# Expert weight products in four column tiles, eight tokens at a time, in a hybrid decoder layer on one core

## The chip, the cores and the metric

The kernel runs on one core of a Trainium2 chip (trn2). The time is device microseconds of one execution, from the first to the last instruction with what lies around them. Three executions of the kernel before took 3187.74, 3201.39 and 3202.97 us, so the median is 3201.39 us. One more execution was profiled.

## The reference

One layer of a decoder trunk is computed for 512 prompt tokens and 64 sample tokens that share all weights: modulation from a condition, an input projection, a gated linear recurrence and a short convolution, an output projection, and then a product-key expert layer (PEER). The change lies in the last. Its core is:

```python
q = (xb @ w_q).reshape(PEER_BLOCK, PEER_HEADS, 2, HALF_DIM)
sc = jnp.einsum('thpk,pnk->thpn', q, sub_keys).astype(jnp.float32)
v1, i1 = lax.top_k(sc[:, :, 0], PEER_TOPK)
v2, i2 = lax.top_k(sc[:, :, 1], PEER_TOPK)
cand = (v1[..., :, None] + v2[..., None, :]).reshape(PEER_BLOCK, PEER_HEADS, PEER_TOPK * PEER_TOPK)
...
top, pos = lax.top_k(cand, PEER_TOPK)
eidx = jnp.take_along_axis(cidx, pos, axis=-1)
g = jax.nn.softmax(top, axis=-1).astype(xb.dtype)
act = jax.nn.gelu(jnp.einsum('td,thkd->thk', xb, expert_u[eidx])) * g
return jnp.einsum('thk,thkd->td', act, expert_v[eidx])
```

Every token picks 8 heads x 16 = 128 of 16384 experts; an expert is a row u and a row v of 2048 numbers. An expert's number is 128 x i1 + i2, so the experts lie in 128 blocks (one per i1) of 128 (one per i2).

## The kernel before

The prompt tokens' picks are treated in two ways. The 80 blocks (L = 80) that are picked most are computed densely: for each such block TensorE multiplies all 128 u rows with all 512 tokens. The picks in the other 48 blocks are gathered: POOL fetches, by an indirect DMA, one row per partition (`take`, L1235), and VectorE takes the dot product of it with the token's vector (L1263), or adds the v row with its weight to a sum (L1290). The sample tokens' picks are gathered too.

**The u stage.** A dense block's u rows come in two halves of 512 KB. `load` (L892) brings a half, `conv` splits it into a high part on ScalarE (xhi, L908) and a low part on POOL (xlo, L909), and `u_half` (L1395) multiplies: 8 slices of the inner dimension, three products each, 24 matmuls of 128 x 512, into one PSUM bank (pu). I call such a half a piece; there are 160, numbered n. After a block's second piece ScalarE applies the gelu and writes the block's activations to DRAM (L1408, L1409). The u banks are two and are taken in turn, so that one of them is idle while the other is filled.

**The weights of the dense picks.** A dense activation must be multiplied by the softmax weight of the token's pick, or by zero where the token did not pick that expert. These weights form, for each token, a matrix of 128 experts by 80 blocks, and TensorE makes it as a product over the token's 128 picks: `g_pair` (L1583) writes with two comparisons on VectorE (L1591), for eight tokens, a one-hot matrix of i2 (ops, 128 x 128) and one of the block (wr, 128 x 80); `g_scale` (L1599) multiplies ops by the picks' weights on ScalarE; `g_mm` (L1601) takes four tokens and makes four products into a PSUM bank (gbank, 4 x 80 columns), and `g_out` (L1608) copies the bank to SBUF on ScalarE (L1612). When 32 tokens are together, four DMAs write them to DRAM (gd); the v stage reads them back (gsb).

**The order.** From the last query projection on, the order on each engine is the one in which the code is written. A loop over the 160 pieces (L1643) writes, for each, the loads and splits of later pieces, one step of the weight work (`g_one`, `g_pair`, `g_scale`), then slot work on VectorE (which tells the rows of the next tile of tokens; steps1 and steps2) as long as a budget named `spare` is positive, then the row fetches and dot products that are due (`gather_to`), and then the matmuls of the piece. `spare` grows by PIECE_G per piece (PIECE before the weight work begins), and falls by 2.4 per row, 2.2 per `g_pair` and by each slot step's own cost. Rows can only be fetched for a tile whose slot work is written; from the piece at which the last slot work is written (R2), all rows that are left are spread evenly over the pieces that remain (L1695). `g_one` is called once at the start of a piece (L1653) and once in its middle, after 12 of its 24 matmuls, by `mid` (L1389, L1402).

**After the u stage** the v stage multiplies the weighted activations (actr, split into ahi and alo) with the v rows of the dense blocks (L1425), while the v rows of the other picks are gathered and added (L1290). Then come the final norm and the output.

## Time and profile before

| what | value |
|---|---|
| median of three runs | 3201.39 us (3187.74 to 3202.97) |
| the profiled execution | 3192.57 us |
| its span, first to last instruction | 3190.7 us |
| TensorE busy | 3063.3 us (96%) |
| VectorE busy | 2151.6 us (67%) |
| ScalarE, POOL busy | 1045.4 us (33%), 1708.0 us (54%) |
| moved by DMA | 882.84 MB, mean 277 GB/s |
| weight products (gbank, L1605) | 1525.5 to 2128.4 us, 1024 records |
| u pieces | up to about 2215 us |

The profile is of one execution. A row of a group gives engine, operation, output and inputs, the count, the busy time and the mean duration in ns, and then the idle time of the engine just before these instructions with what ended it. PE is a matmul and PEld the load of its stationary operand; a product of two f32 operands shows as two of each. Matmuls overlap, so the time from one start to the next tells more than a duration. A row of the timeline gives start and duration of equal neighbours taken together. A row of the waits gives who waited for whom, the sum, the times and the longest. The windows give each engine's busy time in a stretch, then the granted clock, the share of the DMA engines' time and the rate.

### The profile page before, as it was taken

How to read it: one execution, taken by the hardware profiler on the slowest of the kernel's cores; microseconds unless marked ns; L12 is line 12 of the kernel's file. 1: busy time of each engine (PE TensorE's matmuls, PEld its weight loads, DVE VectorE, ACT ScalarE, POOL GpSimd, SP SyncE). 2: the span in 40 equal slices, each digit the busy share in tenths (PEclk: the TensorE clock that was granted, in tenths of full speed). 3: DMA queues.
4: the chain of work that ended last, by engine and by line, in shares of the span. 5: the costliest groups of instructions: out<-in, count | busy, mean ns of one | idle time of the engine just before them, and what ended most of it. 6: DMA issues, size and time to landing. Idle time of an engine off the chain costs nothing.

```text
span 3190.7 us, 46633 instructions
## 1 busy us (share of the span) xinstructions
PE 3063.3 (96%) x17239; PEld 2604.8 (82%) x17239; DVE 2151.6 (67%) x3267; ACT 1045.4 (33%) x1640; POOL 1708.0 (54%) x1001
## 2 busy tenths in 40 slices
PE   6999999999989999999999999998999999999997
PEld 2788888889979998887888788886888888777776
DVE  3455521142245897977898999856677888788755
ACT  3244311122232232232655555542322222222122
POOL 2233333344334235666666666656767777768642
PEclk9999999999999999999999999999999999999998
DMA  9744566633332227889879898989999999899964
GB/s 391 279 137 138 177 215 215 205 121 132 130 121 90 70 83 247 307 312 399 339 309 402 354 400 354 403 281 357 395 376 383 401 341 367 329 397 344 368 245 155
DMA packets 297067, 882.84 MB, mean 277 GB/s; under 512 B 37590, under 2 KB 79446, under 8 KB 245366
## 3 DMA queue, kind: packets, MB, share of 16 engines
q1 hardware_dynamic: 160608, 380.39, 34.0%
q0 software_dynamic: 66336, 413.41, 32.5%
q10 hardware_dynamic: 69888, 86.00, 7.6%
q8 instruction: 136, 2.23, 0.3%
q14 instruction: 99, 0.81, 0.1%
HBM read 879.89 MB, written 66.81 MB: 297 GB/s over the span
## 4 chain that ended last, share of the span: by engine, by line
PE 74%; DMA 12%; DVE 5%; POOL 3%; issue 3%; ACT 1%; SPq 0%; ACTq 0%; POOLq 0%; DVEq 0%
PE pu L1405 20%; PE pv L1425 19%; PE pp_o L140 6%; DMA raw<-v 3%; PE pp_c L140 3%; PE pp_s L140 3%; PE qa L140 3%; PE pp_b L140 3%; PE qb L140 3%; DMA gsb<-gd 3%; PE pp_x L140 2%; PE pp_y L140 2%; PE ada L190 2%; PE gbank L1605 2%; DMA v<-v,rows 2%
## 5 line engine op out<-in xcount | busy, mean ns | idle before, releaser
L909 POOL TENSOR_TENSOR xlo<-raw,xhi 128x1024 fp32r<-128x1024 f32 x320 | 778.6, 2444 | 408.7 <-ACT xhi L908 403.0
L908 ACT ACTIVATE xhi<-raw 128x1024 fp32r<-128x1024 f32 x320 | 338.1, 1060 | 875.4 <-PE pv L1425 319.8
L1263 DVE SCALAR_TENSOR_TENSOR u<-u,hT 128x2048 f32<-128x2048 f32 x223 | 503.7, 2282 | 111.3 <-DMA u<-u,rows 110.0
L1290 DVE SCALAR_TENSOR_TENSOR accB<-v,dots,accB 128x2048 f32<-128x2048 f32 x211 | 496.5, 2353 | 109.4 <-DMA v<-v,rows 103.2
L1425 PE MATMUL pv<-ahi,xhi 128*128 128x512 f32 x1280 | 511.5, 400 | 23.1 <-ACT xhi L908 16.2
L1405 PE MATMUL pu<-hhi,xhi 128*128 128x512 f32 x1280 | 514.4, 402 | 0.0
L1425 PE MATMUL pv<-ahi,xlo 128*128 128x512 f32 x1280 | 508.3, 397 | 4.3 <-POOL xlo L909 4.3
L1425 PE MATMUL pv<-alo,xhi 128*128 128x512 f32 x1280 | 506.0, 395 | 0.0
L1405 PE MATMUL pu<-hhi,xlo 128*128 128x512 f32 x1280 | 502.7, 393 | 0.4 <-POOL xlo L909 0.3
L1405 PE MATMUL pu<-hlo,xhi 128*128 128x512 f32 x1280 | 502.9, 393 | 0.0
L1235 POOL DMA_INDIRECT u<-u,rows x223 | 224.8, 1008 | 211.1 <-DVE u L1263 142.4
L1425 PEld LDWEIGHTS pv<-ahi,xhi 128*128 128x128 f32 x1280 | 243.2, 190 | 80.5 <-ACT xhi L908 17.5
L1425 PEld LDWEIGHTS pv<-ahi,xlo 128*128 128x128 f32 x1280 | 243.1, 190 | 63.0 <-POOL xlo L909 6.2
L1425 PEld LDWEIGHTS pv<-alo,xhi 128*128 128x128 f32 x1280 | 243.6, 190 | 55.2
L1235 POOL DMA_INDIRECT v<-v,rows x223 | 258.1, 1157 | 54.7 <-issue 39.5
L1405 PEld LDWEIGHTS pu<-hhi,xlo 128*128 128x128 f32 x1280 | 240.8, 188 | 56.2 <-POOL xlo L909 2.1
L1405 PEld LDWEIGHTS pu<-hhi,xhi 128*128 128x128 f32 x1280 | 241.4, 189 | 49.4 <-issue 0.9
L1405 PEld LDWEIGHTS pu<-hlo,xhi 128*128 128x128 f32 x1280 | 241.5, 189 | 48.4
L1599 ACT ACTIVATE op<-op,it 128x128 f32<-128x128 f32 x512 | 155.3, 389 | 35.6 <-DVE op L1591 32.8
L1605 PEld LDWEIGHTS gbank<-wr,op 128*128 128x128 f32 x1024 | 133.5, 192 | 24.0 <-ACT stg L1612 15.0
L129 POOL TENSOR_TENSOR wlo_o<-raw_o,whi_o 128x1024 fp32r<-128x1024 f32 x32 | 77.6, 2425 | 119.7 <-ACT whi_o L127 119.7
L1447 DVE TENSOR_TENSOR acc<-acc,pv 128x512 f32<-128x512 f32 x144 | 96.4, 681 | 65.7 <-PE pv L1425 63.6
(498 smaller groups left out, 5439.4 us busy)
## 6 DMA issues: line engine op xcount, KB each, us to landing
wa<-w_ada SPq DMA_DIRECT2D x96, 1024.0 KB
raw<-ut SPq DMA_DIRECT2D x160, 512.0 KB
raw<-v SPq DMA_DIRECT2D x320, 256.0 KB
actd<-act ACTq DMA_DIRECT2D x80, 256.0 KB
gd<-stg ACTq DMA_DIRECT2D x64, 320.0 KB
gsb<-gd ACTq DMA_DIRECT2D x80, 256.0 KB
actr<-actd ACTq DMA_DIRECT2D x40, 512.0 KB
raw_o<-w_out SPq DMA_DIRECT2D x32, 512.0 KB
```

The source lines that it names most:

```text
L129: lo_engine(share).tensor_sub(lo, raw, r32(hi))
L140: PE.matmul(o, st, mv[pick](k), start=first, stop=last)
L908: S.activation(hi, raw, AF.Copy)
L909: G.tensor_sub(lo, raw, r32(hi))
L1235: G.indirect_dma_start(out=out, out_offset=None, in_=src, in_offset=bass.IndirectOffsetOnAxis(ap=idx, axis=0), bounds_check=NE * 128 - 1, ...
L1263: V.scalar_tensor_tensor(r, r, 1.0, st["h"], op0=ALU.mult, op1=ALU.mult, accum_out=dots[i][:, j:j + 1])
L1290: V.scalar_tensor_tensor(st["a"], r, dots[i][:, j:j + 1], st["a"], op0=ALU.mult, op1=ALU.add)
L1405: PE.matmul(pu, st[:, kk, :], movA[mv](k), start=k == 0 and a == 0, stop=k == KD - 1 and a == 2)
L1425: PE.matmul(pv, st, mv, start=first and j == 0 and a == 0, stop=last and not end and j == SG - 1 and a == 2)
L1447: V.tensor_add(ak, ak, pv)
L1599: S.activation(ops[:, j0 + j, :], ops[:, j0 + j, :], AF.Copy, scale=it[2][:, b * 4 + j:b * 4 + j + 1])
L1605: PE.matmul(pg[:, j * L:(j + 1) * L], ops[:, j0 + j, :], wr[:, j0 + j, :], start=True, stop=True)
```

## The change

`g_mm` now takes eight tokens. Each token's product is cut into four: 32 columns of ops are the stationary operand and the result goes to 32 output partitions, 32 products for eight tokens. The first four tokens go to a bank of their own, the u bank that the current block does not use, the other four to gbank. `pbank` names each bank explicitly so that a block and the weight products can ask for one by number. `g_out` copies both banks. `g_one` is no longer called at the start of a piece, only in its middle: after 12 matmuls in a block's first piece as before, after 6 in its second. PIECE_G, the budget per piece, is 6.3 instead of 6.9.

```diff
-PIECE_G = 6.9
+PIECE_G = 6.3
...
-    def pbank(tag, nm, bufs):
-        return psum["p"].tile([128, 512], F32, name=nm, tag=tag, bufs=bufs)
+    turns = {}
+
+    def pbank(tag, nm, bufs, at=None):
+        t = turns.get(tag, 0) if at is None else at
+        turns[tag] = t + 1
+        return psum["p"].tile([128, 512], F32, name=nm, tag=f"{tag}{t % bufs}", bufs=1)
...
-            fin["pu"] = pbank("u", f"pu{i}", 2)
+            fin["pu"] = pbank("u", f"pu{i}", 2, i)
...
-            if kk == 4:
+            if kk == (4, 2)[c]:
                 mid(n)
...
-    def g_mm(b):
-        ops, wr, j0 = pair.pop(b)
-        pg = gk["g"]
-        for j in range(4):
-            PE.matmul(pg[:, j * L:(j + 1) * L], ops[:, j0 + j, :], wr[:, j0 + j, :], start=True, stop=True)
-        return pg
-
-    def g_out(b, pg):
+    def g_mm(b, i):
+        ops, wr, _ = pair.pop(b)
+        pair.pop(b + 1)
+        gk["b"] = (pbank("u", f"gb{b}", 2, i + 1), gk["g"])
+        for j in range(8):
+            pg = gk["b"][j // 4][:, j % 4 * L:(j % 4 + 1) * L]
+            for q in range(0, 128, 32):
+                PE.matmul(pg[q:q + 32], ops[:, j, q:q + 32], wr[:, j, :], start=True, stop=True)
+
+    def g_out(b):
...
-        S.activation(stg[c][:, :, b0 * 4:b0 * 4 + 4].rearrange("p i t -> p t i"),
-                     pg[:, :4 * L].rearrange("p (t i) -> p t i", t=4), AF.Copy)
-        if b0 == TC // 4 - 1:
+        for h_, pg in enumerate(gk["b"]):
+            S.activation(stg[c][:, :, (b0 + h_) * 4:(b0 + h_) * 4 + 4].rearrange("p i t -> p t i"),
+                         pg[:, :4 * L].rearrange("p (t i) -> p t i", t=4), AF.Copy)
+        if b0 == TC // 4 - 2:
...
-        if n >= R1 + FIRST_G and gm[1] < min(upto(n - LAG), gm[2]):
-            g_out(gm[1], g_mm(gm[1]))
-            gm[1] += 1
+        if n >= R1 + FIRST_G and gm[1] + 1 < min(upto(n - LAG), gm[2]):
+            g_mm(gm[1], stream[n][1])
+            g_out(gm[1])
+            gm[1] += 2
             spare += 0.4
...
             put(2)
-            g_one(n)
             if not gk:
```

On TensorE, around the second piece of block 29 and the first of block 30 (pu29, pu30; xhi59 is the high part of piece 59, and the number behind a name is only its place in the program), the order before is:

```order
L1405 MATMUL pu29_14247<-hhi_78,xlo58_14136 128x512
L1605 MATMUL gbank_14007<-wr0_14090,op0_14089 128x80 x4
L1405 MATMUL pu29_14247<-hhi_78,xhi59_14181 128x512
...
L1405 MATMUL pu29_14247<-hhi_78,xlo59_14182 128x512
L1605 MATMUL gbank_14007<-wr0_14090,op0_14089 128x80 x4
L1405 MATMUL pu29_14247<-hhi_78,xhi59_14181 128x512
...
L1605 MATMUL gbank_14007<-wr2_14140,op2_14139 128x80 x4
L1405 MATMUL pu30_14394<-hhi_78,xhi60_14231 128x512
```

and with the change:

```order
L1409 MATMUL pu29_14247<-hhi_78,xlo59_14182 128x512
L1612 MATMUL gb0_14307<-wr0_14090,op0_14089 32x80 x16
L1612 MATMUL gbank_14007<-wr0_14090,op0_14089 32x80 x16
L1409 MATMUL pu29_14247<-hhi_78,xhi59_14181 128x512
...
L1409 MATMUL pu30_14397<-hhi_78,xhi60_14231 128x512
...
L1612 MATMUL gb2_14410<-wr2_14140,op2_14139 32x80 x16
L1612 MATMUL gbank_14007<-wr2_14140,op2_14139 32x80 x16
L1409 MATMUL pu30_14397<-hhi_78,xhi60_14231 128x512
```

Two sets of four tokens, at the start and in the middle of piece 59, became one set of eight after its first six matmuls; the next set comes after the first twelve of piece 60.

On POOL, near the end of the u stage (xlo155 is the low part of piece 155; u5 and v0 are gathered rows of the last tile of tokens and of the samples), the order before is:

```order
L909 TENSOR_TENSOR xlo155_20143<-raw155_20097,xhi155_20142 128x1024
L1235 DMA v0_9_20146<-v,rows0_8654 128x2048
L909 TENSOR_TENSOR xlo156_20190<-raw156_20137,xhi156_20189 128x1024
L1235 DMA v0_10_20193<-v,rows0_8654 128x2048
L1235 DMA v0_11_20198<-v,rows0_8654 128x2048
L909 TENSOR_TENSOR xlo157_20237<-raw157_20184,xhi157_20236 128x1024
L1235 DMA v0_12_20240<-v,rows0_8654 128x2048
L909 TENSOR_TENSOR xlo158_20280<-raw158_20231,xhi158_20279 128x1024
```

and with the change:

```order
L913 TENSOR_TENSOR xlo155_21700<-raw155_21649,xhi155_21699 128x1024
L1239 DMA v0_1_21703<-v,rows0_8654 128x2048
L1239 DMA v0_2_21708<-v,rows0_8654 128x2048
L1239 DMA v0_3_21713<-v,rows0_8654 128x2048
L913 TENSOR_TENSOR xlo156_21760<-raw156_21694,xhi156_21759 128x1024
L1239 DMA v0_4_21763<-v,rows0_8654 128x2048
L1239 DMA v0_5_21768<-v,rows0_8654 128x2048
L913 TENSOR_TENSOR xlo157_21807<-raw157_21754,xhi157_21806 128x1024
L1239 DMA v0_6_21810<-v,rows0_8654 128x2048
L1239 DMA v0_7_21815<-v,rows0_8654 128x2048
L1239 DMA v0_8_21820<-v,rows0_8654 128x2048
L913 TENSOR_TENSOR xlo158_21860<-raw158_21801,xhi158_21859 128x1024
```

The rows that stand between two low parts are two or three instead of one or two. Between xlo151 and xlo161 there are 27 (u5_0 to u5_10 and v0_0 to v0_15) instead of 13 (v0_4 to v0_16). By the planner's own numbers R2 is piece 149 instead of 131.

## The prediction

> **What bounds the kernel now.** I read the chain of waits of the page first, then the windows of the stretch that the change touches, then single instructions. A piece below is one half of a u block: 24 matmuls of L1405 with the work queued around them.
>
> ```profile
> PE 74%; DMA 12%; DVE 5%; POOL 3%; issue 3%; ACT 1%; SPq 0%; ACTq 0%; POOLq 0%; DVEq 0%
> PE pu L1405 20%; PE pv L1425 19%; PE pp_o L140 6%; DMA raw<-v 3%; PE pp_c L140 3%; PE pp_s L140 3%; PE qa L140 3%; PE pp_b L140 3%; PE qb L140 3%; DMA gsb<-gd 3%; PE pp_x L140 2%; PE pp_y L140 2%; PE ada L190 2%; PE gbank L1605 2%; DMA v<-v,rows 2%
> ```
>
> TensorE carries three quarters of the chain, and the matmuls that the change rewrites (gbank, L1605) stand in it with 2%. So a gain is possible, and it is at most some tens of us. Now the stretch with these matmuls (1520 to 2131), the u blocks left after it (2131 to 2215), the v stage, and three stretches inside the first, by the view of windows:
>
> ```profile
> core 0: us, PE busy (x) PEld busy (x) DVE busy (x) ACT busy (x) POOL busy (x), PEclk, DMA share, GB/s
> 1520.00:2131.00 611.00, 601.98 (x3113) 507.29 (x3112) 547.55 (x722) 351.07 (x765) 377.99 (x255) 0.99 0.90 356
> 2131.00:2215.00 84.00, 83.70 (x364) 67.77 (x363) 49.17 (x26) 20.88 (x23) 51.47 (x32) 1.00 0.95 361
> 2215.00:3100.00 885.00, 853.40 (x3662) 690.01 (x3660) 687.15 (x408) 207.53 (x197) 624.91 (x369) 0.98 0.96 361
> 1700.00:1760.00 60.00, 58.44 (x301) 48.33 (x300) 53.78 (x80) 33.85 (x73) 37.76 (x26) 1.00 1.02 420
> 1880.00:1940.00 60.00, 60.00 (x315) 51.06 (x314) 56.00 (x69) 36.36 (x82) 37.27 (x25) 1.00 1.02 421
> 2000.00:2060.00 60.00, 60.00 (x316) 51.06 (x315) 52.35 (x63) 36.48 (x83) 39.32 (x27) 1.00 1.02 419
> ...
> 1940.00:2000.00 60.00, 60.00 (x315) 51.06 (x314) 58.36 (x75) 33.79 (x74) 38.58 (x27) 1.00 0.85 333
> ```
>
> TensorE is busy 602 of 611 us, so it sets the pace. But it is not alone. In three stretches of 60 us the transfers run at 419 to 421 GB/s with a share of 1.02, and I take 421 GB/s as the most that this core gets; between them lie stretches like the last row's, at 333. VectorE is busy 547.6 of 611 us, and the view of waits of the same window says what it does in the rest:
>
> ```profile
> POOL u L1235 <- DVE u L1263: 128.8, 95, 4.3
> DVE u L1263 <- DMA u<-u,rows: 58.4, 40, 6.0
> PEld gbank L1605 <- ACT stg L1612: 15.0, 15, 3.7
> PE gbank L1605 <- ACT stg L1612: 8.9, 11, 3.3
> ```
>
> VectorE waits 58.4 us for gathered rows; 547.6 + 58.4 = 606 of 611, so it has hardly any free time either. POOL waits 128.8 us for VectorE to free a row buffer before it can fetch the next row. TensorE's own idle time, 9 us, is the 8.9 us before gbank. So three chains lie within some 2% of one another in this stretch: TensorE, VectorE with its rows, and in the dense stretches the transfers. What the change gives TensorE has to pass the other two.
>
> **The matmuls themselves.** What four tokens cost now, from the timeline (PE alone):
>
> ```profile
> 1709.04 0.39 PE L1405 MATMUL pu<-hlo,xhi 128*128 128x512 f32 x1
> 1709.27 0.39 PE L1405 MATMUL pu<-hhi,xlo 128*128 128x512 f32 x1
> 1709.50 1.01 PE L1605 MATMUL gbank<-wr,op 128*128 128x80 f32 x8
> 1710.30 0.48 PE L1405 MATMUL pu<-hhi,xhi 128*128 128x512 f32 x1
> 1710.62 0.39 PE L1405 MATMUL pu<-hlo,xhi 128*128 128x512 f32 x1
> ```
>
> A u matmul starts 0.23 us after the one before it (1709.04 to 1709.27). From 1709.27 to 1710.62 there are two such steps, 0.46 us, and the four tokens: 1.35 - 0.46 = 0.89 us. There are 128 such sets (1024 records, 8 a set): 114 us, and eight tokens cost 1.78 us.
>
> The new form, 32 columns of weights into one quarter of the output partitions, is not new to the trace: the ada products have it, with 512 moving columns. Its rows in the timeline, first the matmuls (PE), then the weight loads (PEld):
>
> ```profile
> 411.58 0.60 PE L200 MATMUL pm<-ident,part 128*128 128x128 f32 x4
> 412.11 1.92 PE L190 MATMUL ada<-wa,cpad 128*32 128x512 f32 x16
> 413.97 0.53 PE L140 MATMUL pp_b<-hhi,whi_b 128*128 128x288 f32 x2
> 414.33 0.42 PE L140 MATMUL pp_b<-hlo,whi_b 128*128 128x288 f32 x2
> 414.60 0.42 PE L140 MATMUL pp_b<-hhi,wlo_b 128*128 128x288 f32 x2
> ...
> 412.11 0.16 PEld L190 LDWEIGHTS ada<-wa,cpad 128*32 128x32 f32 x8 [0.17 <-issue]
> 412.57 0.13 PEld L190 LDWEIGHTS ada<-wa,cpad 128*32 128x32 f32 x4 [0.30 <-issue]
> 413.00 0.13 PEld L190 LDWEIGHTS ada<-wa,cpad 128*32 128x32 f32 x4 [0.30 <-issue]
> ```
>
> An f32 product is two passes, so the sixteen records, two products in four tiles each, are four passes of four tiles. The loads of one pass go out 0.43 us after those of the pass before (412.57, 413.00), and all four tiles share that time: they do run side by side. 0.43 us for 512 columns is 0.067 us for 80. Eight tokens are 16 passes (each f32 product has two): 1.07 us. Going in and out of the tiles costs something too. In: the loads idle 0.17 us, of which I count 0.1, and the first pass takes 0.46 instead of 0.43. Out: 413.97 is 0.54 after 413.00 + 0.43, which is 0.11 over a pass, and the next pair takes 0.36 instead of 0.27. That makes 0.33 us, and eight tokens 1.40 us. **Term 1: 64 x (1.78 - 1.40) = 24 us less on TensorE.** Bounds: 45 us less if going in and out cost nothing (64 x 0.71); nothing gained if a pass of short tiles takes as long as a pass of a whole array, 0.89 / 8 = 0.11 us, which 16 times is 1.78 again. I take the value between, since its parts are rows of the same form. No run of tiles in this trace is longer than 16, and here come 64 in a row; that is a rival below.
>
> [...]
>
> **Waits before gbank.** Two banks instead of one, filled once per piece, give ScalarE the rest of a piece to empty them. The cause of the 8.9 us stays, though: the copy (L1612) stands in ScalarE's queue behind the scaling of a later set, and this behind VectorE, which waits for rows. **Term 2: 4 us less** (0 to 9). The rows for this and for what follows: groups of instructions in the stretch with the tiles (two rows), after it (one), and from the page the queue of the gathered rows and their fetches.
>
> ```profile
> L1612 ACT ACTIVATE stg<-gbank 128x320 f32<-128x320 f32 x128 | 97.1, 759 | 14.5 <-PE gbank L1605 11.7 <-issue 2.6
> L1408 ACT ACTIVATE act<-pu 128x512 f32<-128x512 f32 x46 | 27.5, 599 | 121.4 <-PE pu L1405 120.1 <-issue 1.2
> ...
> L1290 DVE SCALAR_TENSOR_TENSOR accB<-v,dots,accB 128x2048 f32<-128x2048 f32 x12 | 28.2, 2354 | 18.1 <-DMA v<-v,rows 18.0
> ...
> q0 software_dynamic: 66336, 413.41, 32.5%
> ...
> L1235 POOL DMA_INDIRECT u<-u,rows x223 | 224.8, 1008 | 211.1 <-DVE u L1263 142.4
> L1235 POOL DMA_INDIRECT v<-v,rows x223 | 258.1, 1157 | 54.7 <-issue 39.5
> ```
>
> In the first half of a block the u bank still holds the block before. The tiles come 12 matmuls, 2.8 us, into the half, and the copy that empties that bank (L1408) takes 0.6 us. In the second half the u bank must be empty before the next block starts, 18 matmuls or 4.1 us after the tiles; two copies at 0.76 us (L1612) fit. Both hold while ScalarE isn't held up by a late row or raw tile; if it is, TensorE waits at the start of a block instead of before gbank. TensorE gets four times as many tile instructions; ScalarE keeps its 128 copies and VectorE its comparisons, and no DMA is added.
>
> **The dense stretches.** Shorter pieces ask for the same two rows in less time. In the three windows at 420 GB/s the transfers can't go faster, so the share of term 1 that falls there is lost: 24 x 180 / 611 = 7 us. **Term 3: 7 us back** (0, if the four rows in flight carry a stretch over, to 15, if the stretches are twice as long as my windows cut them).
>
> **What the smaller PIECE_G moves.** It changes no instruction, but the plan: with 6.3 instead of 6.9 the table grants the slot work less, so tiles of rows come ready later, and the last of them are gathered at the end of the u stage. By POOL's order, between the low halves of pieces 151 and 161 there stand 27 row fetches instead of 13. Those pieces are the 84 us after 2131, where 361 GB/s x 84 us = 30.3 MB move already. A row is 1.05 MB if all 128 partitions are in use; the mean over the kernel is 413.41 MB / 446 row fetches (223 + 223 on L1235) = 0.93 MB. 14 more rows are 13 MB, 43.3 MB in all, and at 421 GB/s 103 us instead of 84. VectorE gets 14 x 2.36 = 33 us more there, 49 + 33 = 82 of 84, so it would just fit; the transfers don't. Does anyone wait for them? The chain of waits, in order of time, says so already for the kernel before:
>
> ```profile
> 2168.09 14.95 DMA v<-v,rows
> 2185.40 2.30 DVE actr L1368
> 2189.26 22.73 DMA gsb<-gd
> 2212.00 9.43 DMA raw<-v
> 2227.04 2.38 POOL xlo L909
> 2229.47 70.59 PE pv L1425 x294
> ```
>
> Rows, then the weights of the next group, then the v columns are what TensorE's first v matmuls wait for; there is no cover left that could hide 13 MB more. The fetches also stand in POOL's queue ahead of the low halves (L909), each waiting for a buffer that VectorE frees, and TensorE waits for those. **Term 4: 103 - 84 = 19 us more** (0, if the rows were hidden, to 36, if the rate stays at 361 GB/s: 13 / 0.361).
>
> **Sum.** -24 - 4 + 7 + 19 = -2 us. The profiled execution took 3192.57 us (span 3190.7, the rest lies around it), so 3190.6 by its own time; it was 8.8 us quicker than the median of the three runs, 3201.39, from which the same sum gives 3199. I put the time between the two, at 3195 us.
>
> **Rivals.** One: *the gain stays*. The mean share of the transfers over the stretch is 0.90, and rows are fetched four ahead; if terms 3 and 4 are hidden, 24 to 45 us remain with up to 9 of the waits. With 33: 3160 us. For it: TensorE is busy 602 of 611 and the sum of VectorE's work falls in the stretch by the 14 rows that leave it. Against: the chain at 2168 to 2229, which has no slack.
>
> Two, the other side: *the rows decide*. Once a piece is shorter than two full rows and its own loads take at 421 GB/s, VectorE waits for every row, its queue holds the scaling, the scaling holds the copies, and TensorE waits before gbank as it did 8.9 us long, now in every dense stretch (15 us); at the end of the u stage the rate stays at 361 GB/s (36 us). 24 less, 51 more: +27, 3220 us. It decides from the point where term 4 exceeds term 1. For it: 606 of 611 on VectorE. Against: between the dense stretches (333 of 421 GB/s) a fifth of the transfers' time is free.
>
> Three: *the tiles don't run side by side in long runs*, so that the change doesn't do what it says. 64 tile passes of 0.067 us one after another are 4.3 us per eight tokens, 2.5 us more, 64 times 160 us: about 3350 us. Against: the 16 that did share their time in the ada rows. [...]
>
> **Chances.** What a measurement can't tell from no change is within 0.5%, 16 us. The forecast, no change: 0.43. Rival one, faster: 0.30. Rival two, slower: 0.20; rival three: 0.07; together slower 0.27. The forecast's own range is 3179 to 3211. For 8 in 10 I go down to 3155, near rival one with its waits, and up to 3235, the case of no gain in term 1 with terms 3 and 4 at 7 and 36 (3192.6 + 43).
>
> **What would show it.** Term 1: groups of 64 tile records with about 1.4 us from the u matmul before to the one after, less 0.23. Term 2: the wait of gbank for stg under 8.9 us. Term 3: windows at 420 GB/s that are no shorter than now, and TensorE busy under 98% in them. Term 4: the u blocks after the last tile set take over 84 us, or the first v matmul waits for over 10 us, with the gsb transfer above 22.7 us. I am wrong if the end of the u stage takes no longer (then rival one), if the stretch with the tiles is not shorter at all (rival two), or if the tile records start more than 0.03 us apart (rival three).

## The result and the profile after

The change made the kernel slower: 3238.0 us (median of 4 runs, 3229.4 to 3242.2) against 3199.4 us (median of 4 runs of the kernel before beside it), a ratio of 1.0116 with an interval of 1.0091 to 1.0141. The prediction was 3195 us, between 3155 and 3235. Two executions in all that follows took 5016 us (g1) and 7641 us (g3) instead of some 3200, and are left out.

I cut both profiled executions at the same instructions, the first matmul of a piece, the end of the last u matmul and the last v matmul:

| stretch | before, us | after, us | difference |
|---|---|---|---|
| up to the first u matmul | 1186.9 | 1189.4 | +2.5 |
| pieces 0 to 57 | 333.2 | 333.4 | +0.2 |
| pieces 58 to 145 (with the weight products) | 616.7 | 608.4 | -8.3 |
| pieces 146 to 159 (the rest of the u stage) | 78.2 | 103.9 | +25.7 |
| v stage, to the last v matmul | 950.7 | 967.3 | +16.6 |
| end | 24.9 | 25.2 | +0.3 |
| span | 3190.7 | 3227.6 | +36.9 |

So the stretch with the tiles became 8 us shorter, where the terms on it made 21, and what comes after it 42 us longer, where the prediction had 19. The 8 us are not the tiles' either: the plan alone, with whole products of four tokens as before, takes 607.0 us there (e2 below), since it moves rows out of the stretch. The lines of the changed kernel are shifted by four to seven: pu is L1409, the weight products (gb, gbank) L1612, their copies L1619, the low halves L913, the row fetches L1239, the dot products L1267, pv L1429. First its chain of waits, from the page:

```profile
PE 73%; DMA 15%; DVE 4%; issue 3%; POOL 3%; ACT 1%; SPq 1%; POOLq 0%; ACTq 0%; DVEq 0%
```

TensorE has 73% of it instead of 74, DMA 15 instead of 12. The view of windows, for the stretch with the tiles, the u blocks after it, the v stage, and the four inner windows that the prediction showed of the kernel before:

```profile
core 0: us, PE busy (x) PEld busy (x) DVE busy (x) ACT busy (x) POOL busy (x), PEclk, DMA share, GB/s
1523.00:2131.00 608.00, 592.89 (x6208) 469.25 (x6207) 506.49 (x674) 352.67 (x767) 362.99 (x240) 0.99 0.87 342
2131.00:2235.00 104.00, 86.01 (x339) 67.25 (x338) 79.57 (x70) 19.70 (x22) 64.34 (x43) 0.92 0.91 344
2235.00:3120.00 885.00, 844.28 (x3598) 682.12 (x3596) 687.09 (x399) 203.01 (x192) 621.47 (x370) 0.97 0.96 359
1700.00:1760.00 60.00, 56.03 (x563) 43.73 (x556) 41.73 (x53) 33.17 (x72) 35.08 (x25) 0.97 0.86 339
1880.00:1940.00 60.00, 57.48 (x649) 45.49 (x648) 48.99 (x93) 34.23 (x75) 34.20 (x23) 1.00 0.80 315
2000.00:2060.00 60.00, 58.66 (x657) 46.49 (x655) 52.64 (x88) 36.51 (x84) 34.35 (x22) 1.00 0.69 254
1940.00:2000.00 60.00, 59.60 (x604) 47.61 (x604) 51.11 (x48) 35.79 (x78) 38.95 (x27) 1.00 1.02 420
```

VectorE fell from 547.6 to 506.5 us in the stretch and rose from 49.2 to 79.6 after it: rows moved to the end, as the order said. The transfers' mean share fell, too, 0.90 to 0.87. So with fewer rows and less work on TensorE the stretch hardly became shorter. Behind it TensorE is busy 86 of 104 us. The view of waits from 2131 to 2300 (who <- for whom: us, times, the longest) tells for whom it waits there:

```profile
PE pu L1409 <- POOL xlo L913: 17.5, 6, 5.7
...
PE pv L1429 <- ACT acc L1449: 10.9, 2, 8.4
```

and in the kernel before, in the same window:

```profile
PE pu L1405 <- POOL xlo L909: 0.3, 1, 0.3
```

The six waits before u matmuls are waits for the low halves, which stand in POOL's queue behind the row fetches. They are 17.5 of the 25.7 us. The other 8 are u matmuls at half the clock, which follow such waits: the granted clock is 0.92 over these 104 us, and was 1.00 before. From the timeline, PE alone, behind one of the waits:

```profile
2154.13 0.50 PE L1409 MATMUL pu<-hhi,xlo 128*128 128x512 f32 x1 [4.13 <-POOL xlo L913]
...
2154.70 0.39 PE L1409 MATMUL pu<-hlo,xhi 128*128 128x512 f32 x1
2154.93 0.40 PE L1409 MATMUL pu<-hhi,xlo 128*128 128x512 f32 x1
...
2155.55 0.63 PE L1409 MATMUL pu<-hlo,xhi 128*128 128x512 f32 x1
2155.98 0.63 PE L1409 MATMUL pu<-hhi,xlo 128*128 128x512 f32 x1
```

A u matmul then starts 0.43 us after the one before it instead of 0.23 (from 2155.2 to 2158.6, where the granted clock is 0.50). Before the v matmuls the longest wait is for a copy on ScalarE (acc, out of the bank of a finished v column), and ScalarE's timeline with its queue (ACTq) shows what holds it, first in the kernel before, then in the changed one:

```profile
2187.73 5.55 ACTq L1356 DMA_DIRECT2D gsb<-gd  x4
...
2228.19 0.99 ACTq L1356 DMA_DIRECT2D gsb<-gd  x2
...
2229.22 1.09 ACTq L1356 DMA_DIRECT2D gsb<-gd  x2
```

```profile
2199.10 11.77 ACTq L1360 DMA_DIRECT2D gsb<-gd  x4
...
2252.62 10.94 ACTq L1360 DMA_DIRECT2D gsb<-gd  x4
...
2276.65 0.60 ACT L1449 ACTIVATE acc<-pv 128x512 f32<-128x512 f32 x1 [12.44 <-DMA gsb<-gd]
```

The weights of the second and third group are asked for 11 and 24 us later than before (the first v matmul comes 20 us later), and to issue the four DMAs takes ScalarE's queue 11.8 and 10.9 us instead of 5.6 and 2.1. The copies that empty the v banks stand behind them. The transfer itself is no longer than it was: 23.2 us in the chain of waits, 22.7 before.

**The tiles.** An undisturbed set of eight tokens, from the timeline (PE alone):

```profile
1590.44 0.39 PE L1409 MATMUL pu<-hhi,xlo 128*128 128x512 f32 x1
1590.76 0.76 PE L1612 MATMUL gb<-wr,op 128*32 128x80 f32 x32
1591.34 0.74 PE L1612 MATMUL gbank<-wr,op 128*32 128x80 f32 x32
1592.01 0.50 PE L1409 MATMUL pu<-hhi,xhi 128*128 128x512 f32 x1
1592.34 0.40 PE L1409 MATMUL pu<-hlo,xhi 128*128 128x512 f32 x1
```

From 1590.44 to 1592.34 are 1.90 us; less two steps of 0.23 that is 1.44 us. The prediction had 1.40. The median of all 64 sets is 1.44 us. But their sum is 117.2 us, not 92, because 15 of the 64 stand still in the middle. The worst, PE alone:

```profile
1711.49 0.39 PE L1409 MATMUL pu<-hhi,xlo 128*128 128x512 f32 x1
1711.81 0.76 PE L1612 MATMUL gb<-wr,op 128*32 128x80 f32 x32
1712.39 0.47 PE L1612 MATMUL gbank<-wr,op 128*32 128x80 f32 x13
1713.24 0.34 PE L1612 MATMUL gbank<-wr,op 128*32 128x80 f32 x4 [0.38 <-issue]
1713.99 0.34 PE L1612 MATMUL gbank<-wr,op 128*32 128x80 f32 x4 [0.41 <-issue]
...
1716.87 0.35 PE L1612 MATMUL gbank<-wr,op 128*32 128x80 f32 x4 [0.49 <-issue]
1718.30 0.58 PE L1409 MATMUL pu<-hhi,xhi 128*128 128x512 f32 x1 [1.09 <-issue]
```

And POOL alone in the same time:

```profile
1712.39 1.00 POOL L1239 DMA_INDIRECT u<-u,rows  x1 [0.30 <-issue]
1713.70 0.99 POOL L1239 DMA_INDIRECT u<-u,rows  x1 [0.31 <-issue]
1715.00 0.99 POOL L1239 DMA_INDIRECT u<-u,rows  x1 [0.30 <-issue]
1716.29 0.99 POOL L1239 DMA_INDIRECT u<-u,rows  x1 [0.30 <-issue]
1717.29 2.38 POOL L913 TENSOR_TENSOR xlo<-raw,xhi 128x1024 fp32r<-128x1024 f32 x1
```

After 45 matmuls the run goes on in handfuls, one to five matmuls and then a gap of 0.6 to 0.7 us, as long as POOL works on row fetches, and the next u matmul comes a microsecond after the last of them. "issue" says that TensorE waited for nothing that the profile shows. I call these the gaps. In the changed kernel they add up to 117.2 - 64 x 1.44 = 25 us, as much as the tiles had saved (128 x 0.89 - 64 x 1.44 = 22).

### The profile page after: what moved, and what is told of

The parts are those of the page before. It is cut to its first block, busy times and chain, and to the rows that moved or that the text cites. A ratio compares the mean times of both kernels' runs of the same rounds, so it can differ in the third digit from the quotient of the medians.

```text
span 3227.6 us, 52817 instructions
## 1 busy us (share of the span) xinstructions
PE 3061.8 (95%) x20311; PEld 2569.9 (80%) x20311; DVE 2150.7 (67%) x3267; ACT 1046.0 (32%) x1640; POOL 1706.4 (53%) x1001
## 4 chain that ended last, share of the span: by engine, by line
PE 73%; DMA 15%; DVE 4%; issue 3%; POOL 3%; ACT 1%; SPq 1%; POOLq 0%; ACTq 0%; DVEq 0%
PE pu L1409 24%; PE pv L1429 14%; DMA raw<-v 6%; PE pp_o L140 6%; DMA gsb<-gd 5%; PE pp_c L140 3%; PE pp_s L140 3%; PE qa L140 3%; PE pp_b L140 3%; PE qb L140 3%; PE pp_x L140 2%; PE pp_y L140 2%; PE ada L190 2%; PE gbank L1612 1%; PE gb L1612 1%
## 5 line engine op out<-in xcount | busy, mean ns | idle before, releaser
L913 POOL TENSOR_TENSOR xlo<-raw,xhi 128x1024 fp32r<-128x1024 f32 x320 | 777.4, 2441 | 429.1 <-ACT xhi L912 422.9
L1267 DVE SCALAR_TENSOR_TENSOR u<-u,hT 128x2048 f32<-128x2048 f32 x223 | 505.6, 2283 | 160.4 <-DMA u<-u,rows 154.1
L1429 PE MATMUL pv<-ahi,xhi 128*128 128x512 f32 x1280 | 512.8, 401 | 30.0 <-ACT xhi L912 12.2
L1409 PE MATMUL pu<-hhi,xlo 128*128 128x512 f32 x1280 | 505.2, 395 | 18.4 <-POOL xlo L913 18.4
L1429 PE MATMUL pv<-ahi,xlo 128*128 128x512 f32 x1280 | 509.9, 398 | 10.7 <-POOL xlo L913 10.7
L1409 PE MATMUL pu<-hhi,xhi 128*128 128x512 f32 x1280 | 513.7, 401 | 2.5 <-issue 1.5
L1429 PE MATMUL pv<-alo,xhi 128*128 128x512 f32 x1280 | 507.3, 396 | 0.0
L1409 PE MATMUL pu<-hlo,xhi 128*128 128x512 f32 x1280 | 506.6, 396 | 0.1
L1239 POOL DMA_INDIRECT u<-u,rows x223 | 224.4, 1006 | 216.3 <-DVE u L1267 168.8
L1429 PEld LDWEIGHTS pv<-ahi,xhi 128*128 128x128 f32 x1280 | 243.9, 191 | 87.8 <-ACT xhi L912 13.8
L1409 PEld LDWEIGHTS pu<-hhi,xlo 128*128 128x128 f32 x1280 | 242.6, 189 | 76.6 <-POOL xlo L913 21.9
L1429 PEld LDWEIGHTS pv<-ahi,xlo 128*128 128x128 f32 x1280 | 244.0, 191 | 70.4 <-POOL xlo L913 13.5
L1239 POOL DMA_INDIRECT v<-v,rows x223 | 258.6, 1160 | 68.3 <-issue 38.0
L1409 PEld LDWEIGHTS pu<-hhi,xhi 128*128 128x128 f32 x1280 | 242.4, 189 | 63.9 <-issue 2.2
L1429 PEld LDWEIGHTS pv<-alo,xhi 128*128 128x128 f32 x1280 | 244.5, 191 | 55.2
L1409 PEld LDWEIGHTS pu<-hlo,xhi 128*128 128x128 f32 x1280 | 242.9, 190 | 52.4 <-issue 1.6
L129 POOL TENSOR_TENSOR wlo_o<-raw_o,whi_o 128x1024 fp32r<-128x1024 f32 x32 | 77.5, 2423 | 119.8 <-ACT whi_o L127 107.5
L1412 ACT ACTIVATE act<-pu 128x512 f32<-128x512 f32 x80 | 47.9, 598 | 278.9 <-PE pu L1409 277.1
```

The lines of the kernel that those rows point to most:

```text
L129: lo_engine(share).tensor_sub(lo, raw, r32(hi))
L913: G.tensor_sub(lo, raw, r32(hi))
L1239: G.indirect_dma_start(out=out, out_offset=None, in_=src, in_offset=bass.IndirectOffsetOnAxis(ap=idx, axis=0), bounds_check=NE * 128 - 1, ...
L1267: V.scalar_tensor_tensor(r, r, 1.0, st["h"], op0=ALU.mult, op1=ALU.mult, accum_out=dots[i][:, j:j + 1])
L1409: PE.matmul(pu, st[:, kk, :], movA[mv](k), start=k == 0 and a == 0, stop=k == KD - 1 and a == 2)
L1429: PE.matmul(pv, st, mv, start=first and j == 0 and a == 0, stop=last and not end and j == SG - 1 and a == 2)
```

## The experiments

All 18 runs, with the median, the ratio to the kernel before in the same comparison and its interval, and from the profiled execution the two stretches, the v stage, the cost of all 64 sets (128 sets of four tokens where there are such), and how many intervals of over 0.3 us there are inside runs of tiles:

| | us | ratio | interval | 58-145 | 146-159 | v | sets | gaps |
|---|---|---|---|---|---|---|---|---|
| before | | | | 616.7 | 78.2 | 950.7 | 127.9 | 0 |
| the change | 3238.0 | 1.0116 | 1.0091-1.0141 | 608.4 | 103.9 | 967.3 | 117.2 | 28 |
| e1 plan undone | 3196.8 | 0.9995 | 0.9973-1.0017 | 603.5 | 84.6 | 964.1 | 93.7 | 0 |
| e2 plan alone | 3226.2 | 1.0116 | 1.0083-1.0149 | 607.0 | 100.6 | 967.3 | 119.8 | 0 |
| e3 whole products | 3226.2 | 1.0099 | 1.0080-1.0118 | 603.9 | 100.2 | 968.9 | 114.4 | 0 |
| e4 two tiles | 3226.2 | 1.0089 | 1.0062-1.0116 | 604.7 | 105.2 | 965.5 | 93.1 | 0 |
| e5 half fetch | 3213.7 | 1.0048 | 1.0029-1.0066 | 619.2 | 83.0 | 940.2 | 114.4 | 19 |
| e6 half dot | 3188.7 | 0.9961 | 0.9935-0.9988 | 603.0 | 82.4 | 967.4 | 114.7 | 26 |
| e7 half fetch, whole | 3212.9 | 1.0045 | 1.0023-1.0067 | 620.2 | 84.1 | 939.4 | 122.0 | 0 |
| e8 the change again | 3241.0 | 1.0129 | 1.0097-1.0162 | 612.2 | 100.7 | 977.2 | 120.8 | 33 |
| g1 half columns | 3192.1 | 0.9987 | 0.9974-1.0000 | 605.6 | 78.9 | 947.2 | 115.6 | 29 |
| g2 half columns, whole | 3183.2 | 0.9955 | 0.9939-0.9970 | 605.8 | 78.5 | 946.9 | 114.3 | 0 |
| g3 even rows | 3192.7 | 0.9990 | 0.9977-1.0002 | | | | | |
| g4 even rows, whole | 3192.5 | 0.9990 | 0.9974-1.0006 | 603.8 | 89.6 | 948.4 | 114.4 | 0 |
| h1 half columns, two tiles | 3181.2 | 0.9940 | 0.9916-0.9963 | 601.3 | 78.1 | 947.7 | 93.4 | 0 |
| h2 even rows, two tiles | 3176.4 | 0.9932 | 0.9908-0.9956 | 584.3 | 88.8 | 948.5 | 93.1 | 0 |
| h3 half columns, two runs | 3193.0 | 0.9976 | 0.9958-0.9994 | 604.8 | 79.0 | 951.5 | 113.6 | 0 |
| i1 even rows, four tiles | 3187.8 | 0.9972 | 0.9957-0.9986 | 589.1 | 90.9 | 955.3 | 103.0 | 12 |
| i2 even rows, two tiles | 3179.0 | 0.9941 | 0.9925-0.9958 | 584.0 | 90.4 | 950.5 | 93.0 | 0 |
| i3 even rows, two runs | 3201.3 | 1.0010 | 0.9996-1.0023 | 601.1 | 89.9 | 959.2 | 114.6 | 1 |

The median is over several executions, the stretches are of one; two executions of one kernel differ by some 10 us in the v stage (967 and 977 for the change). The profiled executions of e1 and e6 took 10 and 15 us more than the median, those of e5 and e7 20 us less.

### The plan and the tiles apart

e1 puts the plan back and keeps the tiles; e2 takes the plan alone.

```diff
 e1, in the changed kernel
-PIECE_G = 6.3
+PIECE_G = 6.9
...
             gm[1] += 2
-            spare += 0.4
+            spare += 0.8
 e2, in the kernel before
-PIECE_G = 6.9
+PIECE_G = 6.3
...
             gm[1] += 1
-            spare += 0.4
+            spare += 0.2
```

> The changed kernel with the budget of the plan put back: PIECE_G 6.9 again, and 0.8 instead of 0.4 granted per set of eight tokens, as two sets of four had it; R2 is then piece 127 (131 before, 149 with the change) and 223 rows are used by piece 145 (225 before, 212 with the change). Theory plan (the smaller budget pushes rows behind the tiles, and that costs 26 us at the end of the u stage and 17 us in the v stage): the pieces 146 to 159 take 78 us again instead of 104, the v stage 976 instead of 992, and the whole 3238 - 43 = 3195 us, about the kernel before. Theory stalls (the long runs of tile matmuls stand still and this is what slows the kernel): the end gains little, 3225 to 3238 us. In both, the 64 groups of tiles still cost about 117 us together.

> The kernel before with only the plan of the change: PIECE_G 6.3 and 0.2 instead of 0.4 granted per set of four tokens, so that R2 is piece 149 and 212 rows are used by piece 145, both as in the changed kernel; TensorE's work is untouched. Theory plan: 3199 + 26 + 17 = 3242 us, pieces 146 to 159 at 104 us, v stage at 992 us. Theory stalls: 3199 us, within 0.5%.

The plan theory held in the whole, and at the end of the u stage. With the plan undone the kernel takes the time of the kernel before (0.9995), and the end of the u stage is 84.6 us. The plan alone, with TensorE's work untouched, costs 1.16%, as much as the whole change, and the 100.6 and 967.3 us stand where those of the change do. In its waits from 2122 to 2300 the same rows appear:

```profile
PE pu L1405 <- POOL xlo L909: 13.6, 6, 4.6
...
PE pv L1425 <- ACT acc L1445: 11.0, 2, 9.1
```

In the v stage it held only at the start. The first twelfth of the v matmuls takes 104 to 107 us in the five executions with the smaller budget (the change twice, e2, e3, e4) and 80 to 95 in all others, e1 among them with 94.5. But e1's whole v stage was expected 16 us shorter than the change's and is 3 us shorter (964.1 against 967.3): waits later in it are longer there, as in some other executions with either plan. The wait for ScalarE's copies is not the plan's alone either: e1 has 9.3 us of it (10.9 in the change), and there, too, one issue of the gsb DMAs takes ScalarE's queue some 10 us. So the plan is shown to cost some 10 to 16 us at the start of the v stage; which wait makes the difference is not.

What both theories said of the tiles was wrong: in e1 the 64 sets cost 93.7 us, with no gap in any of them. The saving was there, 34 us against the kernel before (127.9). But the stretch is only 13 us shorter, 603.5 against 616.7, and 30.7 of the 603.5 us are waits before u matmuls (by this I mean, here and below, all that the steps from one u matmul to the next take beyond 0.23 us; in e3 it is 9.2). The two stretches behind it took 6 and 13 us more than in the kernel before, and nothing was left.

e3 and e4 keep the change's plan and alter the product:

```diff
-            for q in range(0, 128, 32):
-                PE.matmul(pg[q:q + 32], ops[:, j, q:q + 32], wr[:, j, :], start=True, stop=True)
 e3
+            PE.matmul(pg, ops[:, j, :], wr[:, j, :], start=True, stop=True)
 e4
+            for q in range(0, 128, 64):
+                PE.matmul(pg[q:q + 64], ops[:, j, q:q + 64], wr[:, j, :], start=True, stop=True)
```

> The changed kernel with each token's product whole again (128 columns of weights in one matmul, 8 products for eight tokens instead of 32); banks, places and plan as in the change. If the tiles saved nothing because their runs stand still (64 sets cost 117 us, as much as whole products cost before), this takes the time of the changed kernel, 3238 us within 0.3%, the groups cost 1.78 us each, and no gap of 0.6 us stands in them. If the tiles did gain their 24 us and something else lost them, it is slower, about 3260 us.

> The changed kernel with two column tiles of 64 instead of four of 32: 16 products for eight tokens, 32 matmul records in a run instead of 64, the rest as in the change. Theory supply (a long run uses up the instructions that stand ready, after 39 to 62 records, and TensorE then waits for more): no gap of 0.6 us in any group, 64 sets cost as the undisturbed ones did, 1.44 us, 92 us together, and the kernel gains 25 us against the change, 3213 us. If two tiles do not run side by side as four do, a set costs 2.5 us or more and the kernel takes 3300 us. If the gaps have nothing to do with the number of matmuls, they come in about 20 groups again and the time stays 3238 us.

e3 is as expected where the tiles saved nothing. e4 is half right: two tiles do run side by side, a set costs 1.45 us, and there is no gap, as expected of half the instructions (though e1 has none with all of them); but the 25 us did not arrive: 1.0089 and 1.0099 can't be told apart. The view of waits of e4 in its stretch (1523 to 2127) says where they went:

```profile
ACT xhi L912 <- DMA raw<-ut: 54.2, 30, 5.2
...
PE pu L1409 <- POOL xlo L913: 9.5, 8, 3.7
...
PE pu L1409 <- ACT stg L1619: 7.9, 6, 1.8
```

TensorE waits for low halves (9.5 us), these for the high halves (53.9 us, POOL xlo <- ACT xhi), and these for raw weights that arrive late (54.2 us); or for ScalarE's copies (7.9 us). In e3, e4 and e1 the stretch is 603.5 to 604.7 us whether a set costs 1.78 or 1.45 us. So a second thing held the stretch, and it was to be found.

### Transfers, VectorE, or the gaps

```diff
 all in e1, for rows of u fetched from piece 53 on
 e5, e7: 64 of the 128 partitions
-            take(held[j][0], A["u"], rows_i[i][:, j:j + 1])
+            take(held[j][0][:64], A["u"], rows_i[i][:64, j:j + 1])
 e6: 1024 of the 2048 columns in the dot product
-            V.scalar_tensor_tensor(r, r, 1.0, st["h"], ...)
+            V.scalar_tensor_tensor(r[:, :m], r[:, :m], 1.0, st["h"][:, :m], ...)
 e7: and whole products as in e3
```

> Four tiles, budget put back (the first experiment), and from piece 53 on the row fetches of u bring 64 of the 128 partitions, with the dot product on those 64 (an instruction on 64 partitions takes VectorE as long as one on 128); half of the picks' activations are left out of the result. TensorE's own work in pieces 58 to 145 is 88 x 24 x 0.229 + 64 x 1.44 = 575 us; with the full rows these pieces took 603.5 us, 30.7 of them waits before u matmuls. Theory transfers (these waits come from transfers that can't go faster): 575 to 582 us, and the whole 22 to 28 us under the first experiment, 3170 us. Theory VectorE (its queue of dot products and comparisons paces the pieces): 600 us or more, the whole 3197 us.

> Four tiles, budget put back, and from piece 53 on the dot products of u rows go over 1024 of the 2048 columns, which leaves half of each product out of the result; the rows are fetched whole. VectorE has some 1.2 us less per row. Theory transfers: pieces 58 to 145 at 600 us or more, the whole about 3195 us, as in the first experiment. Theory VectorE: 575 to 582 us, the whole about 3170 us.

> As the experiment with half of the fetched rows, but with whole products instead of four tiles: sets of 1.78 us, TensorE's own work in pieces 58 to 145 is 483 + 114 = 597 us. Theory transfers: with the rows halved TensorE sets the pace, so this takes 22 us longer than the same with four tiles: 597 to 604 us in these pieces, the whole about 3192 us. Theory VectorE: both take the same.

> The changed kernel, unaltered, beside these experiments. If the gaps of 0.6 us within the runs of tiles belong to the kernel, about 20 of the 64 groups have one again and the groups cost about 117 us; if they belonged to that one execution, there are few, the groups cost about 95 us, and the waits stand before the u matmuls instead, 25 to 32 us in pieces 58 to 145. The time is 1.0 to 1.4% over the kernel before in both cases.

e5 and e7 tell nothing of that question, since their edit did not do what it was meant to: the pieces took longer, not less. The row of the gathered rows' queue in the view of the DMA, of e1 and then of e5, both from 1520 to 2120 (queue, packets, MB, share of 16 engines):

```profile
q0 software_dynamic: 23406, 138.90, 57.0%
```

```profile
q0 software_dynamic: 13069, 78.12, 48.7%
```

A packet took 0.570 x 16 x 600 / 23406 = 0.234 us and now 0.487 x 16 x 600 / 13069 = 0.358: with half the partitions each packet took half as long again, and the raw weights came later still (ScalarE waits 89.9 us for them, 53.3 in e1). VectorE gained nothing by it: it was busy 537.6 of the 600 us with 154 rows asked for, and 547.9 us with 157 in e1, so a dot product on 64 partitions took it about as long as one on 128.

e6 is inconclusive in the whole and telling in its parts. VectorE fell from 548 to 385 us of 600, and the waits before u matmuls from 30.7 to 9.1. But now the tiles have gaps, the sets cost 114.7 us instead of 93.7, and the stretch is 603.0 again. The profile is of one of six executions at 3188 to 3204 us; the other four took 3175 to 3181, near the 3170 of theory VectorE, and whether they had gaps is not known.

e8 says that the gaps belong to the kernel: 33 of them, 120.8 us.

Then the row's width instead of its partitions, with tiles (g1), whole products (g2) and two tiles (h1):

```diff
 in e1
+                take(held[j][0][:, :D // 2], A["u"].rearrange("e (a k) -> (e a) k", a=2), rows_i[i][:, j:j + 1])
...
+                for _ in range(2):
+                    V.scalar_tensor_tensor(r[:, :D // 2], r[:, :D // 2], 1.0, st["h"][:, :D // 2], ...)
```

> Four tiles, budget put back, and from piece 53 on a row fetch of u brings 1024 numbers for each of the 128 partitions instead of 2048 (half of another expert's row, so the activations of these picks are not the reference's); VectorE works as long as before, with two dot products of 1024. The fetch on 64 partitions did not test what it was meant to: the rate fell from 363 to 259 GB/s and the transfers' share stayed at 0.96. Theory transfers: with half the bytes on all partitions the waits go, and pieces 58 to 145 take TensorE's own 575 us and a little, 575 to 585, against 603.5 with full rows. Theory supply (the runs of tiles stand still for want of instructions): about 20 groups with gaps, as when the dot products were halved, and 600 us or more.

> The same with whole products instead of four tiles; TensorE's own work in pieces 58 to 145 is 597 us. Theory transfers: 597 to 604 us, that is 20 us more than with the tiles. Theory supply: the same time as with the tiles, 597 to 604 us both.

The rate fell to 251 GB/s at a share of 0.75, so transfers held nobody here. The four tiles have 29 gaps and take 605.6 us, the whole products 605.8: this looked like the gaps alone. It is not clean, though: the two halves of a dot product made VectorE busier (566 and 572 of 600 us), and h1, the same with two tiles and no gap, had 28.5 us of waits in place of the gaps:

> Half of each fetched row of u as in the experiment with half columns (so these activations are not the reference's), and two column tiles of 64 instead of four of 32: 64 instructions in a run instead of 128 (matmuls and weight loads), the same PE time for the passes. Theory supply: the gaps of 0.6 us in 21 of 64 groups of the four-tile version go, the sets take 1.44 us, and pieces 58 to 145 take 481 + 92 + 11 = 584 us instead of 605.6, the whole some 3165 to 3175 us. Rival (something else holds these pieces at 604 us, whatever TensorE has to do): 600 us or more again, with waits before u matmuls in place of the gaps.

601.3 us is the rival's number. With half rows VectorE is the likely next bound: in h1 it is busy 575 of 600 us, and ScalarE waits 77.1 us for its comparisons (9.6 in g1). No run tests that.

### Rows spread evenly

The way out was to take the pressure from transfers and VectorE alike. The kernel's plan asks for two rows per piece until the ready ones are used up, and then for none; with 1.8 per piece the pauses nearly go.

```diff
 in e1; g4 with whole products, h2 and i2 with two tiles, g3 and i1 with four
-RATE = (1.0, 2.0)
+RATE = (1.0, 1.8)
```

> Four tiles, budget put back, and rows asked for at 1.8 instead of 2.0 per piece (RATE): 218 rows are used by piece 145 instead of 223, 26 instead of 21 after it, and the pieces without rows are 59 and 60 only (58 to 60, 78 and 79 with 2.0). Per piece of 6.54 us these are 1.8 x 0.93 + 0.52 + 0.35 = 2.55 MB, 390 GB/s, under the 421 that this core gets. Theory transfers: TensorE sets the pace in pieces 58 to 145, 575 to 590 us instead of 603.5; the pieces after them take up to 11 us more for five rows; the whole 3175 to 3190 us. Theory supply: 600 us or more, the whole about 3200 us.

> The same plan of rows with whole products: 597 to 605 us in pieces 58 to 145, the whole about 3197 us. Theory transfers: some 15 to 20 us more than with four tiles. Theory supply: no difference.

> Whole rows, spread evenly (RATE 1.8), budget put back, two column tiles of 64. With whole products this plan took 603.8 us in pieces 58 to 145 and 3192.5 us in all. Theory supply: no gaps, 582 to 592 us in these pieces, the whole 3172 to 3182 us, 0.5% under the kernel before. Rival: transfers hold the pieces at 600 us or more, the whole 3190 us.

> Rows spread evenly (RATE 1.8), budget put back, four tiles of 32 columns. Theory supply: some 20 groups with gaps of 0.6 us, the 64 groups at 112 to 118 us instead of 93, pieces 58 to 145 at 600 to 606 us, the whole at 3192 us and 0.5% over two tiles. Rival (transfers and VectorE held the earlier four-tile versions, gaps came from that): no gaps, 582 to 590 us, as fast as two tiles.

> The same with two tiles of 64 columns, again, beside the four: 584 us in pieces 58 to 145, no more than 3 groups with gaps, the whole at 0.993 of the kernel before.

There is no usable profile of g3; i1 is the same kernel again. The windows of pieces 58 to 145 and of 146 to 159, of whole products (g4), four tiles (i1) and two tiles (h2), in this order:

```profile
1523.70:2127.50 603.80, 600.93 (x3137) 510.78 (x3136) 535.92 (x713) 355.76 (x772) 375.45 (x252) 1.00 0.90 354
2127.50:2217.10 89.60, 81.10 (x338) 64.63 (x337) 55.51 (x36) 19.47 (x22) 54.20 (x36) 0.96 0.98 374
```

```profile
1525.10:2114.20 589.10, 584.15 (x6209) 465.91 (x6208) 529.11 (x709) 351.76 (x765) 373.10 (x250) 1.00 0.91 361
2114.20:2205.10 90.90, 81.57 (x338) 64.66 (x337) 55.52 (x36) 19.64 (x22) 55.38 (x36) 0.96 0.97 374
```

```profile
1525.60:2109.90 584.30, 580.92 (x4162) 465.50 (x4161) 535.69 (x710) 351.56 (x766) 373.57 (x250) 1.00 0.92 364
2109.90:2198.60 88.70, 80.92 (x337) 64.21 (x335) 55.10 (x37) 19.18 (x22) 52.97 (x35) 0.96 0.99 381
```

Here the saving arrives: 603.8 to 584.3 us with two tiles, 19.5, against 114.4 - 93.1 = 21.3 us of TensorE's time. The whole is 0.9932 and 0.9941 of the kernel before, 19 to 22 us faster than it and some 60 faster than the change. The even plan with whole products, in the banks and places of the change, gives next to nothing (g4, 0.9990): it takes 13 us from the stretch and gives 11 back behind it. Four tiles lie between: 12 gaps, 103.0 us for the sets, 589.1 us. My expectation for i1 was too high (600 to 606) and its rival's too clean (no gap at all); 9.9 of the 21 us were lost in gaps, not all of them.

### The length of a run

```diff
 h3 (on g1) and i3 (on i1)
         for j in range(8):
+            if j == 4:
+                yield          # nine u matmuls later the other four tokens
```

> Half of each fetched row of u, four tiles, but the eight tokens in two runs of four, nine u matmuls apart: as many instructions as with one run, each run half as long; going in and out of the tiles is paid twice, some 0.35 us more per set. If the length of a run matters (a stock of instructions is used up within it): no gaps of 0.6 us, 128 groups of 0.9 us, pieces 58 to 145 at about 607 us. If the mean number of instructions per time matters: gaps as before, 20 us more, about 627 us.

> The same plan with four tiles in two runs of four tokens, nine u matmuls apart; 128 groups instead of 64, in and out of the tiles twice. If the length of a run matters: hardly any gap, 0.89 us per group, 128 x 0.89 = 114 us, pieces 58 to 145 at 480 + 114 + 10 = 604 us, the whole 3192 us. If the mean number of instructions per time matters: gaps stay, about 625 us, the whole 3210 us.

As many instructions, runs half as long: one gap of over 0.3 us in 256 runs, where g1 and i1 have gaps in 24 of 128. So the length of a run matters, not the mean number of instructions. The sets cost 113.6 and 114.6 us nonetheless, since the way in and out of the tiles is paid twice: two runs take 2 x 0.89 = 1.78 us, one takes 1.44, so in and out cost 0.34 us.

## Why the prediction was wrong

The forecast of no change was 21 us less (terms 1 to 3) and 19 more (term 4), and both halves failed. Of the 21 us nothing arrived: with the plan undone the tiles leave the time where it was (e1, 0.9995). And the plan costs more than 19: alone it makes the kernel 1.16% slower (e2), 30 us by the medians and 37 by the ratio.

**What bounds the kernel.** The reading was right that three chains lie close together. I didn't take it to its end: if they lie within 2%, a gain on one of them is at most what the others leave, and that is small.

**Term 1, 24 us less on TensorE.** The size of a set was right, 1.44 us against 1.40, and with two tiles 64 sets cost 93 us, 21 less than whole products. In the changed kernel the sum was 117.2 us, since 15 of the 64 runs stood still in the middle. The step of this term that failed is the one from a run of 16 tile matmuls to one of 64, of which I said that no run so long was in the trace and that it was a rival. Rival three was right that long runs are another matter, and wrong in its mechanism and price: the tiles do run side by side, 64 starts lie within 1.08 us, 0.017 us apart on average.

**Term 2, 4 us less waiting before gbank.** Right in direction and too small: the waits for the copies are gone altogether (8.9 us before). In the runs without gaps other waits take their place, 7.9 us before u matmuls in e4, as the working said they would if ScalarE is late.

**Term 3, 7 us back in the dense stretches.** A second chain took the saving back, as the term said, but the term was mis-sized. With the plan undone or with two tiles all of the saving came back as waits before u matmuls (e1: 30.7 us, e4: 32.3, against 9.2 in e3 with whole products), some 22 us instead of 7. I had charged only the share of the saving that falls into three windows of 420 GB/s, 180 of 611 us. The kernel before runs at 400 GB/s or more in 22 of 40 slices of 15 us from 1520 to 2120, which is 330 us, and by the same rule 13 us back; they are no more with the faster TensorE (21 in e1). So the share was read too small, and the rule is too mild besides. Whether transfers or VectorE's queue hold it there is not separated: e6 relieved VectorE and e5 did not relieve the transfers, and the even plan relieves both (in h2 ScalarE waits 28.7 us for raw weights and 33.9 for VectorE's comparisons, in e1 53.3 and 64.3).

**Term 4, 19 us for rows moved behind the tiles.** Right in kind, as e2 and e1 show: 25.7 us in the change's profile, 22.4 with the plan alone, within the bounds of 0 to 36. That the u blocks take 104 us, where I had 103, is luck. My sum was bytes at 421 GB/s, and the rate there fell, from 361 to 344: some 36 MB moved in the 104 us, not 43, at a share of 0.91. Of the two ways that I gave, rows for VectorE and fetches in POOL's queue ahead of the low halves, the second one shows: six waits, 17.5 us, and some 8 us of matmuls at half the clock behind them, for which I had no term. What I missed is the v stage, 16.6 us. I had said that there is no cover left before the first v columns, and then counted the delay of the u stage only. It was neither the first v matmul nor a longer gsb transfer, as I had put it. The first twelfth of the v matmuls took 104.4 us instead of 89.2, and that is 15 of the 16.6. The longest wait in it stands behind the DMAs of gsb, which hold ScalarE's queue some 11 us, twice, so that the v banks are not emptied; that this wait is what the plan added is argued and not shown, since e1 has most of it. Terms by measurement: -8 for the stretch, +26, +17, and 3 elsewhere, where I had -21 and +19. My upper bound of 3235 had nothing for the v stage, and charged term 3 where it left no gain to lose; that the time came out only 3 us above it is luck.

I also gave the cause of the later rows to PIECE_G alone. The halved number of calls halves what the table gets back per call of the weight work, too: e2 has both, and R2 is piece 149 with them; no run has one without the other.

**The rivals.** Rival two, the rows decide, is the nearest: its +27 us has the point right, term 4 above what is left of term 1. Its waits before gbank did not come. Rival one holds only where the rows are spread (h2), with 20 us.

**What would show it.** The set at 1.4 us, the shorter waits before gbank and the u blocks over 84 us came as described; the sign at the first v matmul did not. The stretches at 420 GB/s were read from windows at fixed times, and there the rate is 254 to 339 GB/s now, because the dense phases have moved; that sign could not be read.

## What to carry to other kernels

Where several chains lie within a few per cent, take what a faster engine frees and ask, stage by stage, what the others leave of it; the saving showed only when the rows' demand was evened out first. A number in a planner is a change of its own: time it alone, and follow what it moves past the end of its stage into the next. A wait of TensorE can cost more than its length, as here, where matmuls at half the clock, 0.43 us apart instead of 0.23, followed it: 17.5 us of waits, and some 8 us more behind them. And before a long run of short instructions is written, try a shorter one: half as many tiles, of twice the width, cost the same time here, 1.45 against 1.44 us a set, and had no gap of over 0.3 us (e4, h1, h2, i2).

## What the runs showed of the hardware that I had not expected

**Long runs of short TensorE instructions can stand still while POOL works on a row fetch.** They do in six of seven executions. A run of 64 tile matmuls has 128 instructions with its weight loads. In five executions with such runs (the change twice, e6, g1, i1: 320 runs) 76 have an interval of over 0.3 us, and in all 76 POOL is at work on a fetch during the run's 1.44 us; in the 169 runs without one there is no such interval. Where a fetch begins between 0.12 us before and 0.76 us after a run's start, all 72 runs have an interval of over 0.15 us. In a sixth, e5, all 9 such runs have one, and 11 of its 12 runs with an interval of over 0.3 us have a fetch at work; before the twelfth a fetch had just ended. A case of one fetch in the changed kernel, from the timeline of all engines:

```profile
1645.14 0.76 PE L1612 MATMUL gb<-wr,op 128*32 128x80 f32 x32
1645.26 1.00 POOL L1239 DMA_INDIRECT u<-u,rows  x1 [0.63 <-DVE u L1267]
...
1645.72 0.45 PE L1612 MATMUL gbank<-wr,op 128*32 128x80 f32 x13
1646.57 0.61 PE L1612 MATMUL gbank<-wr,op 128*32 128x80 f32 x19 [0.41 <-issue]
```

The pause begins about 0.7 us after the fetch and ends 1.3 us after it. In 1.08 us TensorE works through 128 instructions, 119 per us; by that rate 0.7 us are some 80, an estimate. Runs of 32 matmul records, 64 instructions, had no gap but one (h3, i3, and two tiles in e4, h1, h2, i2), though in 123 of them a fetch begins in that same interval.

So runs of 128 instructions can have gaps, and runs of 64 have all but none, as theory supply has it. What holds TensorE up in them was not shown, though: the profile says only "issue", and no run takes the fetches away. The theory is a reading of these counts.

The seventh execution speaks against a plain rule: e1 has 18 fetches that begin in that same interval, and no gap at all. One of them, from its timeline:

```profile
1808.84 0.76 PE L1612 MATMUL gb<-wr,op 128*32 128x80 f32 x32
1809.11 1.00 POOL L1239 DMA_INDIRECT u<-u,rows  x1 [4.62 <-DVE u L1267]
...
1809.41 0.74 PE L1612 MATMUL gbank<-wr,op 128*32 128x80 f32 x32
```

What was different there the runs do not tell; it stays open.

**Two column tiles of 64 cost as much as four of 32**: 1.45 and 1.44 us for eight tokens with 80 moving columns, against 1.78 for whole products, with half the instructions of the four.

**A gather over 64 partitions is no cheap gather**: its packets took 0.358 us (e5) instead of 0.234 (e1).
